# A third PSUM bank for the recurrences of the second segment, and B's serial products queued behind A's

## The chip, the core and the metric

The kernel runs on one core of a Trainium2 chip. The metric is the device time of one execution in microseconds (us), median of three runs. The core's engines work beside each other, each through a queue of its own and in the order in which its instructions stand there: TensorE (PE, matrix products; its weight loads are shown apart as PEld), VectorE (DVE), ScalarE (ACT), GpSimd (POOL), and SyncE (SP), which only issues transfers. PE writes its results to PSUM, eight banks of 128 x 512 f32; DVE and ACT empty them.

## The reference

A decoder block over 16 meta tokens and 1024 tokens of width 1024. `mm` stands for a product with weights, all in float32:

```python
h = concat(meta, x)
h = h + 0.5 * swiglu(rmsnorm(h), w_gu, w_down)             # D 1024, hidden 2816
u = rmsnorm(h)
aq, ak, av, az, beta, alpha, bcols, ga, gb = split(u @ w_in)
o_a = gated_delta(...)   # 8 heads of 128: per chunk  v_new = u - w S;  o = q S + attn v_new
                         #                            S = S * exp(g) + k^T v_new
o_b = rwkv7(...)         # 16 heads of 64: S = S * w + (S a) b + v k;   y = S r
h = h + (sigmoid(ga) * o_a + sigmoid(gb) * o_b) @ w_out
h = h + 0.5 * swiglu(rmsnorm(h), w_gu2, w_down2)
out = rmsnorm(h)[meta:]
```

A is the gated DeltaNet branch, B the RWKV-7 branch. Both carry a state from token to token; the kernel brings them to a form in which the state moves from chunk to chunk, 128 tokens for A and 64 for B.

## The kernel before

Three stages follow each other: `ffn1`, `middle` (from about 880 us to 2400 us of the span) and `ffn2`. Large products are made of three products of split operands (`mm3`): a projection tile `pp` of 128 x 512 takes 8 x 3 = 24 matmuls with a bank of PSUM, and its weights `w` come as `wraw` by a transfer and are split in two by ACT (L159) and DVE (L160). The small products of the recurrences are in plain f32; the trace shows each of those as two matmuls of half the length, with two weight loads.

`middle` runs two segments: the first of 528 tokens (the 16 meta tokens and 512), the second of 512. In each it takes eight pairs of heads, one of A with two of B. So there are 16 iterations, it 0 to 7 and 8 to 15. In an iteration the function `schedule` lists, in this order: `merge_blocks` and `transitions` (what B's chunks and the triangular inverses need, products iv, xp, vp, mp, np), `operands` of the next iteration (grb, gra, bkt, ktp), its inverse (62 small DVE steps, tb and Xb), `chains`, `gates` (projections zg, gs, gg and the product gat), `finish` (column sums cs, norms, merge), and `new_b` and `new_a` two iterations ahead (projections vB, kB, rB; column sums cs and bon; the meta tokens' transpose vbm in segment 1; convolutions acc). This is the programme's order only: a scheduler draws instructions from all these acts into each engine's queue, with the earlier act first where several are ready by its own reckoning. What stands in a queue is then fixed, and an instruction that waits holds all behind it. In the second half of it 6 the banks are dealt anew for segment 2 (`segment`), so the work from it 7 on runs with the second segment's banks.

The eight banks of `middle` are three pools: mm (projections), mx (operands and column sums of new work) and ch (`merge_blocks`, `transitions`, `chains` and `finish`'s column sums). ch has two banks throughout; mm has two tiles of two banks in segment 1 and three of one bank in segment 2; mx has the rest, two and three.

`chains` walks the states. For a chunk i of A: p1 (state times keys) goes to DVE, which makes rhA; p2 (inverse times rhA) goes to ACT, which makes vn; pq gathers two products, pq1 with the state and pq2 with vn, and ACT copies it to kq; p3 (keys times vn) goes to DVE, which makes the new state S (the tile SA). For a chunk of B: b (transition times state) goes to DVE, which makes the next state, a slice of SBs. Four chunks of A and eight of B follow one after another, and after them bq makes B's outputs of all chunks. Each product takes the next bank of ch, in program order; the next bank has to be empty. In the program before, the chunks stand as b0, A0, b1, b2, A1, b3, b4, A2, b5, b6, A3, b7.

`transitions` forms its products with `run`, which fills two tiles (even and odd chunks), each a bank: `mp` is emptied by DVE into mt (four steps, L1472) and AR (two, L1475), xp by ACT into xa, xv (L1464) and at, `np` by DVE into vbk and yb.

Of the kernel before, what the change touches and what calls it, by code (L numbers as in the profile page):

```python
# [13 lines left out]
P = 128  # L14
# [14 lines left out]
NCB = FULL // CB  # L29
CA = 128  # L30
NCA = FULL // CA
# [7 lines left out]
NJ = 8  # L39
WB = 2  # L40
AHEAD = 1
S1 = 3
HK = KD // 2
HF = NF // 2
NTMP = 8
# [61 lines left out]
def build(tc, nc, a):  # L107

    ctx = ExitStack()
    with ctx:  # L110
        g = K()
        g.tc, g.nc, g.a = tc, nc, a
        nc.scalar.preload_act_table_set("natural_log_exp_and_others")
        pad = ctx.enter_context(tc.tile_pool(name="pad", bufs=1, side="right"))
        nc.vector.memset(pad.tile([P, 24], F32, name="pad"), 0.0)
        const = ctx.enter_context(tc.tile_pool(name="const", bufs=1))
        wp = ctx.enter_context(tc.tile_pool(name="wp", bufs=2))
        dram = ctx.enter_context(tc.tile_pool(name="dram", bufs=1, space=bass.MemoryType.DRAM))
        g.mmctx = ctx.enter_context(ExitStack())
        main_banks(g, 2, 3, 8)  # L120
        g.const, g.wp, g.dram = const, wp, dram

        ones = const.tile([P, P], F32, name="ones")
        nc.gpsimd.dma_start(ones, a["ck"][:, :P])
        g.pk = const.tile([P, NPK], F32, name="pk")
        nc.gpsimd.dma_start(g.pk, a["pk"])

        def pv(n):
            o, w = PK[n]
            return g.pk[:, o : o + w]  # L130

        nc.vector.tensor_scalar(pv("omu"), pv("mu"), -1.0, 1.0, op0=ALU.mult, op1=ALU.add)
        nc.vector.tensor_scalar(pv("oka"), pv("ka"), -1.0, 1.0, op0=ALU.mult, op1=ALU.add)
        for n in ("w0", "a0"):
            nc.vector.tensor_scalar(pv(n), pv(n), -1.0, None, op0=ALU.mult)
        g.C = lambda n: ones if n == "ones" else g.ck[:, CK[n][0] - P : CK[n][0] - P + CK[n][1]]
        g.V = lambda n, i=0: g.pk[:, PK[n][0] + i : PK[n][0] + i + 1]

        hdr = [dram.tile([KD, P, sn], F32, name=f"hdr{s}") for s, (_, sn, _) in enumerate(SEGS)]
        mdr = [dram.tile([NJ, P, FULL], F32, name=f"mdr{s}") for s in range(2)]  # L140
        g.hdr, g.mdr = hdr, mdr
        g.sdr = dram.tile([NJ, P, P + CB], F32, name="sdr")
        g.gdr = [dram.tile([NJ, FULL], F32, name=f"gdr{s}") for s in range(2)]
        g.rdr = dram.tile([P, FULL], F32, name="rdr")
        g.h2dr = dram.tile([KD, P, FULL], F32, name="h2dr")
        g.h3dr = dram.tile([KD, P, FULL], F32, name="h3dr")
        g.hid = dram.tile([NF, P, T], F32, name="hid")

        g.worder, g.wready, g.wfetched, g.wused = list(weight_order()), [], 0, 0
        ffn1(g)  # L150
        middle(g)
        ffn2(g)
# [83 lines left out]
    return w  # L236


def main_banks(g, w, n, banks=6):

    g.mmctx.close()
    g.mmw = w
    pool = lambda name, bufs: g.mmctx.enter_context(
        g.tc.tile_pool(name=name, bufs=bufs, space=bass.MemoryType.PSUM, reuse_waits="tile"))
    g.mm = pool("mm", n)
    g.mx = pool("mx", banks - n * w)


def mm_tile(g, name, n=512, first=256):
# [462 lines left out]
def ffn2(g):  # L712
    tc, nc = g.tc, g.nc
    n = FULL
    main_banks(g, 1, 6, 8)
    with ExitStack() as ctx:
        right = ExitStack()
        bp = ctx.enter_context(tc.tile_pool(name="f2b", bufs=1, reuse_waits="tile"))
# [2 lines left out]
        with tc.tile_pool(name="f2n", bufs=1, reuse_waits="tile") as sp:  # L721
# [16 lines left out]
            w = next(q0), next(q1)  # L738
# [44 lines left out]
def middle(g):  # L783
    tc, nc = g.tc, g.nc
    g.mmctx.close()
    with ExitStack() as ctx:
        g.ch = ctx.enter_context(tc.tile_pool(name="ch", bufs=2, space=bass.MemoryType.PSUM, reuse_waits="tile"))
        ctx.callback(g.mmctx.close)
        ep = lambda name, bufs=1: ctx.enter_context(tc.tile_pool(name=name, bufs=bufs, reuse_waits="tile"))
        g.ms = ep("ms")  # L790
        g.st = ep("st")
        ms = g.ms
        g.carB = ms.tile([P, 27], F32, name="carB")
        g.carA = ms.tile([P, 24, 3], F32, name="carA")
        g.nrate = ms.tile([P, 1], F32, name="nrate")
        nc.scalar.activation(g.nrate[64:72], g.V("lr")[64:72], AF.Exp)
        nc.vector.tensor_scalar(g.nrate[64:72], g.nrate[64:72], -1.0, None, op0=ALU.mult)


        g.Y = [ms.tile([P, NT, P], F32, name=f"Y{i}") for i in range(2)]  # L800
        g.XA = ms.tile([CB, NCA, 2, 2, 16], F32, name="XA")
        g.Ub = ms.tile([115, 32, 32], F32, name="Ub")

        g.mt = ms.tile([P, NCB, P], F32, name="mt")
        for t in (*g.Y, g.XA, g.Ub, g.mt):
            nc.gpsimd.memset(t, 0.0)
        g.bkpm = ms.tile([P, 2, 64], F32, name="bkpm")
        nc.gpsimd.memset(g.bkpm, 0.0)
        g.bkm = ms.tile([P, 64], F32, name="bkm")
        nc.gpsimd.memset(g.bkm, 0.0)  # L810

        g.upz = ms.tile([P, 4, P], F32R, name="upz")
        nc.gpsimd.memset(g.upz.bitcast(F32), 0.0)
        g.uvm = [ms.tile([64, P], F32, name=f"uvm{i}") for i in range(2)]
        for t in g.uvm:
            nc.gpsimd.memset(t, 0.0)


        g.sums = {}
        for x in ("ones", "bd"):  # L820
            g.sums[x] = ms.tile([P, P], F32R, name=f"{x}r")
            nc.vector.tensor_copy(g.sums[x], g.C(x))
        steps = {}
        for act, it in schedule():
            if act == "segment":
                segment(g, it)
            elif act == "new_b":
                steps[it] = new_b(g, it)
            else:
                ACTIONS[act](g, steps[it])  # L830
# [24 lines left out]
def segment(g, s):  # L855

    nc = g.nc
    t0, n, off = SEGS[s]
    if s:
# [3 lines left out]
        for k in range(KD):  # L863
# [1 line left out]
            nc.sync.dma_start(hk[:, :n], g.hdr[s][k])  # L865
            nc.vector.scalar_tensor_tensor(hk[:, :n], hk[:, :n], g.V("gm", k), rs[:, :n], op0=ALU.mult, op1=ALU.mult)
            g.u.append(u_tile(g, hk[:, :n]))
    main_banks(g, *((1, S1) if s else (2, 2)))
    c = g.seg = K()
    c.s, c.n, c.off, c.u = s, n, off, g.u  # L870
    lora(g, c)
# [612 lines left out]
def chains(g, q):  # L1484
# [34 lines left out]
    def chunk_a(i):  # L1519
        csl = slice(i * CA, (i + 1) * CA)  # L1520
        p1 = pt("p1")
        nc.tensor.matmul(p1[:, :P], lhsT=kqg[:, 0, csl], rhs=S, start=True, stop=True)
        rh = st.tile([P, P], F32, name="rhA", tag="rhA", bufs=1)
        nc.vector.tensor_tensor(rh, Va[:, i, :], p1[:, :P], op=ALU.subtract)
        p2 = pt("p2")
        nc.tensor.matmul(p2[:, :P], lhsT=Y[:, NCB + i, :], rhs=rh, start=True, stop=True)
        vn = st.tile([P, P], F32, name="vn", tag="vn", bufs=2)
        nc.scalar.activation(vn, p2[:, :P], AF.Identity, scale=c.tk[:, i, j : j + 1])
        pq = pt("pq")
# [7 lines left out]

    SBs = st.tile([P, NCB + 1, CB], F32, name="SBs", tag="SBs")
    nc.gpsimd.tensor_copy(SBs[:, 0], SB)
    for i in range(NCB):  # L1540
        ps = pt("b1")
        nc.tensor.matmul(ps[:, :CB], lhsT=g.mt[:, i], rhs=SBs[:, i], start=True, stop=True)  # L1542
        nc.vector.scalar_tensor_tensor(SBs[:, i + 1], ps[:, :CB], q.gam[:, i : i + 1], q.vbk[:, i],
                                       op0=ALU.mult, op1=ALU.add)
        if i % 2 == 0:
            chunk_a(i // 2)
    ps = pt("bq")
    for i in range(NCB):
        for hp in HS:
# [146 lines left out]
```

## Time and profile before

| | us |
|---|---|
| three runs, median | 3086.55 (3084.68 to 3089.25) |
| profiled execution | 3085.29 |
| its span, first to last instruction | 3083.5 |
| PE busy | 2959.3 (96%) |
| DVE busy | 1976.2 (64%) |
| ACT busy | 1376.7 (45%) |
| POOL busy | 354.9 (12%) |

PE is busy nearly throughout, so the span is PE's work and the short stretches in which PE waits. Its clock was granted at 0.989 of full speed on average. Busy shares are means over stages that differ: DVE is busier in `middle` than before and after it.

### The profile page before, as it was taken

The numbers are of one execution on the slowest core, as the hardware profiler recorded it, in microseconds if no ns is written. First come the engines' busy times: TensorE is split into PE (matmuls) and PEld (weight loads), VectorE is DVE, ScalarE is ACT, GpSimd is POOL, SyncE is SP. The second block draws the span as 40 slices with busy tenths as digits, with TensorE's granted clock in tenths as the row PEclk, the third lists the DMA queues.
The fourth block names the chain that finished last, engine by engine and source line by source line (L and its number), as shares of the span: only waits on it lengthen the run. The fifth ranks groups of instructions, "written<-read, shape, count | busy, mean of one in ns | idle before, by whom it ended". The sixth has DMA issues, their size and how long they took to land.

```text
span 3083.5 us, 61656 instructions
## 1 busy us (share of the span) xinstructions
PE 2959.3 (96%) x25498; PEld 2539.0 (82%) x25498; DVE 1976.2 (64%) x3840; ACT 1376.7 (45%) x2404; POOL 354.9 (12%) x519
## 2 busy tenths in 40 slices
PE   8999999999899999999999999999999999999998
PEld 8999998998778888788777777777777888887886
DVE  6455454346677777787867877777866655555335
ACT  5322222126555656566566655665644432222114
POOL 0222220000001000001001000010100022222000
PEclk9999999999899999999999999999999999999999
DMA  3232224234222322333332332223354232224223
GB/s 125 82 97 83 83 86 158 79 101 140 62 74 73 79 70 59 85 79 75 97 89 73 84 81 75 75 75 84 109 148 165 68 104 94 83 83 170 86 78 114
DMA packets 257593, 287.19 MB, mean 93 GB/s; under 512 B 169296, under 2 KB 175440, under 8 KB 257312
## 3 DMA queue, kind: packets, MB, share of 16 engines
q1 hardware_dynamic: 253072, 271.43, 29.4%
q0 software_dynamic: 2512, 8.65, 0.7%
q8 instruction: 201, 3.29, 0.4%
q10 hardware_dynamic: 1728, 3.16, 0.3%
q14 instruction: 80, 0.66, 0.1%
HBM read 232.70 MB, written 50.47 MB: 92 GB/s over the span
## 4 chain that ended last, share of the span: by engine, by line
PE 54%; DVE 11%; ACT 7%; issue 2%; DMA 2%; SPq 0%; DVEq 0%; POOL 0%; ACTq 0%
PE pp L262 18%; PE pg L450 12%; PE pd L262 7%; PE pwo L262 3%; DVE w L160 1%; PE pg L474 1%; PE b L1542 1%; PE cs L1003 1%; PE gra L1252 1%; DMA ugr<-in_upg 1%; PE bkt L1281 1%; DVE tb L1364 1%; DVE mt L1472 1%; DVE Xb L1366 1%; PE vp L1056 1%
## 5 line engine op out<-in xcount | busy, mean ns | idle before, releaser
L262 PE MATMUL pp<-uk,w 128*128 128x512 f32 (+2 forms) x4824 | 975.1, 347 | 15.8 <-DVE w L160 9.3
L262 PEld LDWEIGHTS pp<-uk,w 128*128 128x128 f32 x4824 | 744.7, 191 | 109.1 <-DVE w L160 13.0
L159 ACT ACTIVATE w<-wraw 128x1024 fp32r<-128x1024 f32 (+2 forms) x330 | 326.3, 989 | 712.6 <-PE pd L262 287.6
L262 PE MATMUL pd<-hd,w 128*128 128x512 f32 (+2 forms) x2640 | 495.6, 349 | 11.3 <-DVE w L160 6.7
L262 PEld LDWEIGHTS pd<-hd,w 128*128 128x128 f32 x2640 | 427.5, 189 | 78.2 <-DVE w L160 8.6
L160 DVE TENSOR_TENSOR w<-wraw,w 128x1024 fp32r<-128x1024 f32 (+2 forms) x330 | 376.1, 1140 | 90.9 <-ACT w L159 85.7
L456 DVE TENSOR_TENSOR c<-c,pg 128x520 f32<-128x520 f32 (+1 forms) x280 | 189.2, 689 | 337.3 <-PE pg L450 278.3
L450 PE MATMUL pg<-bt,w 128*128 128x256 f32 (+2 forms) x2520 | 403.9, 317 | 0.0
L450 PEld LDWEIGHTS pg<-bt,w 128*128 128x128 f32 x2520 | 361.0, 188 | 32.9 <-DVE w L160 0.2
L450 PE MATMUL pg<-b,w 128*128 128x256 f32 (+2 forms) x2160 | 348.1, 317 | 0.2 <-DVE c L456 0.2
L450 PEld LDWEIGHTS pg<-b,w 128*128 128x128 f32 x2160 | 309.8, 188 | 28.5 <-PE pg L450 0.4
L419 POOL TENSOR_TENSOR wrx<-wrx 128x512 f32<-128x512 f32 x38 | 57.2, 1505 | 755.1 <-DVE w22b L160 515.3
L1364 DVE TENSOR_TENSOR tb<-Ub,Xb 115x126 f32<-115x126 f32 (+22 forms) x496 | 124.1, 250 | 11.0 <-DMA Ub<-scr 2.7
L1366 DVE TENSOR_TENSOR Xb<-Xb,tb 115x126 f32<-115x126 f32 (+22 forms) x496 | 125.3, 253 | 8.7
L159 ACT ACTIVATE w<-wrx 128x1024 fp32r<-128x1024 f32 (+1 forms) x64 | 58.1, 908 | 156.8 <-PE pg L450 152.3
L1173 DVE SCALAR_TENSOR_TENSOR acc<-xr,pk,acc 128x528 f32<-128x528 f32 (+1 forms) x144 | 109.0, 757 | 26.4 <-ACT acc L1169 25.3
L609 DVE SCALAR_TENSOR_TENSOR h<-pd,h 128x528 f32<-128x528 f32 (+1 forms) x64 | 44.6, 698 | 115.0 <-PE pd L262 115.0
L609 DVE SCALAR_TENSOR_TENSOR hh<-pd,hh 128x512 f32<-128x512 f32 x64 | 44.2, 690 | 109.7 <-PE pd L262 106.6
L262 PE MATMUL pwo<-uk,w 128*128 128x512 f32 x384 | 101.5, 414 | 4.2 <-DVE w L160 1.9
L262 PEld LDWEIGHTS pwo<-uk,w 128*128 128x128 f32 x384 | 73.6, 197 | 22.2 <-DVE w L160 2.7
L923 ACT ACTIVATE sh<-pp,pk 128x528 f32<-128x528 f32 (+1 forms) x54 | 37.5, 694 | 98.3 <-PE pp L262 98.3
L159 ACT ACTIVATE hd<-hr 128x1040 fp32r<-128x1040 f32 (+1 forms) x44 | 45.3, 1061 | 68.6 <-DMA hr<-hid 43.7
(397 smaller groups left out, 4143.1 us busy)
## 6 DMA issues: line engine op xcount, KB each, us to landing
wraw<-in_win SPq DMA_DIRECT2D x150, 512.0 KB
wraw<-in_wgu SPq DMA_DIRECT2D x44, 512.0 KB
wrx<-in_wgu SPq DMA_DIRECT2D x44, 512.0 KB
wraw<-in_wdn SPq DMA_DIRECT2D x48, 320.0 KB
wraw<-in_wdn SPq DMA_DIRECT2D x32, 384.0 KB
hid<-c SPq DMA_DIRECT2D x44, 260.0 KB
hr<-hid SPq DMA_DIRECT2D x22, 520.0 KB
hid<-c SPq DMA_DIRECT2D x44, 256.0 KB
```

Source lines behind the costliest of these rows:

```text
L159: g.nc.scalar.activation(hi, src, AF.Copy)
L160: (eng or g.nc.vector).tensor_tensor(lo, src, hi.bitcast(F32), op=ALU.subtract)
L262: g.nc.tensor.matmul(ps, lhsT=l, rhs=r, start=i == 0, stop=i == n - 1)
L419: sums.tensor_tensor(a22, a21, a22, op=ALU.add)
L450: nc.tensor.matmul(ps[:, c0 : c0 + cn], lhsT=l[:, x, k, :], rhs=r[:, k, y, c0 : c0 + cn], start=i == 0, stop=i == 3 * HK - 1)
L456: nc.vector.tensor_tensor(o, x, y, op=ALU.add)
L474: nc.tensor.matmul(ps[:, c0 : c0 + cn], lhsT=l[:, x, k, :], rhs=r[:, k, y, c0 : c0 + cn], start=i == 0, stop=i == 6 * HK - 1)
L609: nc.vector.scalar_tensor_tensor(hv, pd, 0.5, hv, op0=ALU.mult, op1=ALU.add)
L923: nc.scalar.activation(sh[:, 1 : 1 + n], ps, AF.Identity, scale=g.V("mu", i))
L1173: nc.vector.scalar_tensor_tensor(acc[:, :n], xr[:, tap : tap + n], V("convw", ct * 4 + tap), acc[:, :n], op0=ALU.mult, op1=ALU.add)
L1364: nc.vector.tensor_tensor(tv, U[:, i, i + 1 :].unsqueeze(2).to_broadcast([npt, nt, ncc]), X[:, i, 0:ncc].unsqueeze(1).to_broadcast([npt, n ...
L1366: nc.vector.tensor_tensor(X[:, i + 1 :, 0:ncc], X[:, i + 1 :, 0:ncc], tv, op=ALU.add)
```

## The change

Three things are edited. The ch pool is made in `main_banks`, with mm and mx, and so can differ by segment. In segment 2 it gets three banks, and mm two (`S1` 3 to 2); segment 1 keeps two tiles of mm, two banks of mx and two of ch, in other places. In `chains` the body of B's loop becomes `chunk_b`, and the chunks' products are put by `issue_after`: b of chunk 2i directly behind p1 of A's chunk i, b of chunk 2i+1 directly behind p2. No product and no transfer is added or taken away.

```diff
--- before.py
+++ after.py
@@ -39,7 +39,7 @@
 NJ = 8
 WB = 2
 AHEAD = 1
-S1 = 3
+S1 = 2
 HK = KD // 2
 HF = NF // 2
 NTMP = 8
@@ -117,7 +117,7 @@
         wp = ctx.enter_context(tc.tile_pool(name="wp", bufs=2))
         dram = ctx.enter_context(tc.tile_pool(name="dram", bufs=1, space=bass.MemoryType.DRAM))
         g.mmctx = ctx.enter_context(ExitStack())
-        main_banks(g, 2, 3, 8)
+        main_banks(g, 2, 3)
         g.const, g.wp, g.dram = const, wp, dram
 
         ones = const.tile([P, P], F32, name="ones")
@@ -236,14 +236,16 @@
     return w
 
 
-def main_banks(g, w, n, banks=6):
+def main_banks(g, w, n, ch=0):
 
     g.mmctx.close()
     g.mmw = w
     pool = lambda name, bufs: g.mmctx.enter_context(
         g.tc.tile_pool(name=name, bufs=bufs, space=bass.MemoryType.PSUM, reuse_waits="tile"))
     g.mm = pool("mm", n)
-    g.mx = pool("mx", banks - n * w)
+    g.mx = pool("mx", 8 - n * w - ch)
+    if ch:
+        g.ch = pool("ch", ch)
 
 
 def mm_tile(g, name, n=512, first=256):
@@ -712,7 +714,7 @@
 def ffn2(g):
     tc, nc = g.tc, g.nc
     n = FULL
-    main_banks(g, 1, 6, 8)
+    main_banks(g, 1, 6)
     with ExitStack() as ctx:
         right = ExitStack()
         bp = ctx.enter_context(tc.tile_pool(name="f2b", bufs=1, reuse_waits="tile"))
@@ -784,7 +786,6 @@
     tc, nc = g.tc, g.nc
     g.mmctx.close()
     with ExitStack() as ctx:
-        g.ch = ctx.enter_context(tc.tile_pool(name="ch", bufs=2, space=bass.MemoryType.PSUM, reuse_waits="tile"))
         ctx.callback(g.mmctx.close)
         ep = lambda name, bufs=1: ctx.enter_context(tc.tile_pool(name=name, bufs=bufs, reuse_waits="tile"))
         g.ms = ep("ms")
@@ -865,7 +866,7 @@
             nc.sync.dma_start(hk[:, :n], g.hdr[s][k])
             nc.vector.scalar_tensor_tensor(hk[:, :n], hk[:, :n], g.V("gm", k), rs[:, :n], op0=ALU.mult, op1=ALU.mult)
             g.u.append(u_tile(g, hk[:, :n]))
-    main_banks(g, *((1, S1) if s else (2, 2)))
+    main_banks(g, *((1, S1, 3) if s else (2, 2, 2)))
     c = g.seg = K()
     c.s, c.n, c.off, c.u = s, n, off, g.u
     lora(g, c)
@@ -1519,11 +1520,15 @@
     def chunk_a(i):
         csl = slice(i * CA, (i + 1) * CA)
         p1 = pt("p1")
-        nc.tensor.matmul(p1[:, :P], lhsT=kqg[:, 0, csl], rhs=S, start=True, stop=True)
+        m = nc.tensor.matmul(p1[:, :P], lhsT=kqg[:, 0, csl], rhs=S, start=True, stop=True)
         rh = st.tile([P, P], F32, name="rhA", tag="rhA", bufs=1)
         nc.vector.tensor_tensor(rh, Va[:, i, :], p1[:, :P], op=ALU.subtract)
+        with g.tc.issue_after(m.ins):
+            chunk_b(2 * i)
         p2 = pt("p2")
-        nc.tensor.matmul(p2[:, :P], lhsT=Y[:, NCB + i, :], rhs=rh, start=True, stop=True)
+        m = nc.tensor.matmul(p2[:, :P], lhsT=Y[:, NCB + i, :], rhs=rh, start=True, stop=True)
+        with g.tc.issue_after(m.ins):
+            chunk_b(2 * i + 1)
         vn = st.tile([P, P], F32, name="vn", tag="vn", bufs=2)
         nc.scalar.activation(vn, p2[:, :P], AF.Identity, scale=c.tk[:, i, j : j + 1])
         pq = pt("pq")
@@ -1537,13 +1542,15 @@
 
     SBs = st.tile([P, NCB + 1, CB], F32, name="SBs", tag="SBs")
     nc.gpsimd.tensor_copy(SBs[:, 0], SB)
-    for i in range(NCB):
+
+    def chunk_b(i):
         ps = pt("b1")
         nc.tensor.matmul(ps[:, :CB], lhsT=g.mt[:, i], rhs=SBs[:, i], start=True, stop=True)
         nc.vector.scalar_tensor_tensor(SBs[:, i + 1], ps[:, :CB], q.gam[:, i : i + 1], q.vbk[:, i],
                                        op0=ALU.mult, op1=ALU.add)
-        if i % 2 == 0:
-            chunk_a(i // 2)
+
+    for i in range(NCA):
+        chunk_a(i)
     ps = pt("bq")
     for i in range(NCB):
         for hp in HS:
```

The scheduler draws the whole order of `middle` anew. Three places show what changes.

The first is PE's queue in it 12, in `chains`: one chunk of A with its two chunks of B. Before:

```order
L1542 MATMUL b_23890<-SBs,mt 128x64 [waits Activation_49]
L262 MATMUL pp<-uk,w 128x512 x4
L1542 MATMUL b_23893<-SBs,mt 128x64 [waits DVE_49]
L1522 MATMUL p_23896<-SA,kq 128x128
L262 MATMUL pp<-uk,w 128x512 x3
L1526 MATMUL p_23900<-rhA,Y_7138 128x128 [waits DVE_49]
L1530 MATMUL pq<-kq,SA 128x128
L262 MATMUL pp<-uk,w 128x512 x2
L1531 MATMUL pq<-attn,vn 128x128 [waits Activation_49]
L1533 MATMUL p_23907<-vn,ktl 128x128
L262 MATMUL pp<-uk,w 128x512
```

And now:

```order
L1523 MATMUL p_23897<-SA,kq 128x128 [waits DVE_49,Activation_49]
L1548 MATMUL b_23901<-SBs,mt 128x64
L264 MATMUL pp<-uk,w 128x512 x2
L1529 MATMUL p_23904<-rhA,Y_7135 128x128 [waits DVE_49]
L1548 MATMUL b_23906<-SBs,mt 128x64 [waits DVE_49]
L1535 MATMUL pq<-kq,SA 128x128
L264 MATMUL pp<-uk,w 128x512
L1536 MATMUL pq<-attn,vn 128x128 [waits Activation_49]
L1538 MATMUL p_23914<-vn,ktl 128x128
L264 MATMUL pp<-uk,w 128x512 x3
```

There were four visits between projections (b; b and p1; p2 and pq1; pq2 and p3), now there are three. Counted over the sixteen iterations, such visits are 263 before (118 up to it 6, 145 from it 7 on) and 221 now (112 and 109). The projections between p1 and p2 are two instead of three.

The second is PE's queue in it 12, at the end of `transitions`, where grb and gra are operands of the next iteration. Before:

```order
L1056 MATMUL mp<-BKt,xa 64x64 [waits Activation_49]
L1056 MATMUL mp<-BKt,xa 64x64 x7
L1056 MATMUL mp<-LT,xa 64x64 x12
L1211 MATMUL grb<-AR,BK 64x128 x15
L262 MATMUL pp<-uk,w 128x512 x2
L1056 MATMUL np<-xv,BKt 64x64 [waits DVE_49,PE_49]
L1056 MATMUL np<-xv,BKt 64x64 x2
L1056 MATMUL np<-xv,BKt 64x64 [waits DVE_49,PE_49]
L1056 MATMUL np<-xv,BKt 64x64 x12
L1056 MATMUL np<-LT,xv 64x64 x16
L1211 MATMUL grb<-AR,BK 64x128 [waits DVE_49]
L1211 MATMUL grb<-AR,BK 64x128 x7
```

And now:

```order
L1057 MATMUL mp<-BKt,xa 64x64 [waits Activation_49]
L1057 MATMUL mp<-BKt,xa 64x64 x7
L1057 MATMUL mp<-LT,xa 64x64 x13
L1057 MATMUL np<-xv,BKt 64x64 [waits Activation_49]
L1057 MATMUL np<-xv,BKt 64x64 x7
L1057 MATMUL np<-LT,xv 64x64 x8
L1212 MATMUL grb<-AR,BK 64x128 x8
L1057 MATMUL np<-xv,BKt 64x64 [waits DVE_49,PE_49]
L1057 MATMUL np<-xv,BKt 64x64 x7
L1057 MATMUL np<-LT,xv 64x64 x8
L1212 MATMUL grb<-AR,BK 64x128 x11
```

The first half of np, which had stood with the second behind fifteen grb and two projections, stands directly behind mp; eight grb separate the halves.

The third is PE's queue in it 7, from the last column sum of `finish` and `new_b` to bon and beyond, where the queue of `new_a` follows. Before:

```order
L1003 MATMUL cs<-hl,bdr 128x512
L262 MATMUL pp<-uk,w 128x512 x4
L1003 MATMUL cs<-hl,bdr 128x512
L262 MATMUL pp<-uk,w 128x512 x27
L1003 MATMUL bon<-hl,bdr 128x512 x2
L262 MATMUL pp<-uk,w 128x512 x17
L1003 MATMUL cs<-hl,onesr 128x512
L262 MATMUL pp<-uk,w 128x512 x4
L1003 MATMUL cs<-hl,onesr 128x512
L262 MATMUL pp<-uk,w 128x512 x18
```

And now:

```order
L1004 MATMUL cs<-hl,bdr 128x512
L264 MATMUL pp<-uk,w 128x512 x3
L1004 MATMUL cs<-hl,bdr 128x512
L264 MATMUL pp<-uk,w 128x512 x5
L1004 MATMUL bon<-hl,bdr 128x512
L264 MATMUL pp<-uk,w 128x512 x3
L1004 MATMUL bon<-hl,bdr 128x512
L264 MATMUL pp<-uk,w 128x512 x31
L1004 MATMUL cs<-hl,onesr 128x512
L264 MATMUL pp<-uk,w 128x512 x5
```

Between the end of `chains` (bq) and the first bon product stood 58 projection matmuls, now 35; behind it come 17, now 3 and 31, until the next column sum. On DVE's queue three weight splits (L160) stood between the first rhA of it 7 and bv, of which bon's operand is made; now one.

In segment 1, its 1 to 7, vbm stood on PE behind vbp and two projection matmuls of 272 columns; now it stands behind vbp and eight of them.

## Rows read from the trace of the kernel before

**Rows 1.** The page's first part: busy us (share) and instructions.

```profile
PE 2959.3 (96%) x25498; PEld 2539.0 (82%) x25498; DVE 1976.2 (64%) x3840; ACT 1376.7 (45%) x2404; POOL 354.9 (12%) x519
```

**Rows 2.** PE's waits, whole run: waiting line <- releaser: us in total, times, longest.

```profile
PE np L1056 <- DVE AR L1475: 14.1, 15, 2.3
...
PE vbm L1118 <- ACT Vs L1115: 6.3, 8, 1.0
PE vp L1056 <- ACT xv L1464: 6.0, 14, 0.6
...
PE p L1526 <- DVE rhA L1524: 2.2, 1, 2.2
```

**Rows 3.** Its 8 to 14 as one window: us, busy by engine, PEclk, DMA.

```profile
core 0: us, PE busy (x) PEld busy (x) DVE busy (x) ACT busy (x) POOL busy (x), PEclk, DMA share, GB/s
1681.18:2284.11 602.93, 579.78 (x6497) 463.90 (x6496) 479.49 (x1131) 354.32 (x680) 48.45 (x104) 1.00 0.33 88
```

**Rows 4.** Waits of line 1542 (b), whole run: releaser, us, times.

```profile
  ACT kq L1535: 10.7, 47
```

**Rows 5.** Timeline of it 12, one A chunk: start, us, instruction, idle before.

```profile
2146.34 0.30 PEld L1542 LDWEIGHTS b<-SBs,mt 128*128 128x128 f32 x2 [0.23 <-ACT kq L1535]
...
2146.59 1.17 PE L262 MATMUL pp<-uk,w 128*128 128x512 f32 x4
...
2147.60 0.33 PE L1542 MATMUL b<-SBs,mt 128*128 128x64 f32 x2
...
2147.77 0.44 PE L1522 MATMUL p<-SA,kq 128*128 128x128 f32 x2
...
2147.96 0.94 PE L262 MATMUL pp<-uk,w 128*128 128x512 f32 x3
...
2148.24 0.29 DVE L1524 TENSOR_TENSOR rhA<-Va,p 128x128 f32<-128x128 f32 x1
...
2149.10 0.71 PE L262 MATMUL pp<-uk,w 128*128 128x512 f32 x2
2149.16 0.37 ACT L1528 ACTIVATE vn<-p,tk 128x128 f32<-128x128 f32 x1 [2.86 <-PE p L1526]
...
2150.43 0.43 PE L1542 MATMUL b<-SBs,mt 128*128 128x64 f32 x2
```

**Rows 6.** Timeline of PE, segment 1, around vbm.

```profile
1324.83 4.39 PE L262 MATMUL pp<-uk,w 128*128 128x272 f32 x35
...
1331.29 0.39 PE L1118 MATMUL vbm<-ck,vB 128*16 128x128 f32 x2 [1.00 <-ACT Vs L1115]
```

**Rows 7.** Timeline of it 12, end of the transitions.

```profile
2133.39 1.73 DVE L1472 TENSOR_TENSOR mt<-mp,ck 64x256 f32<-64x256 f32 x4 [0.21 <-PE mp L1056]
...
2135.14 0.76 DVE L1475 TENSOR_TENSOR AR<-mp,AR 128x256 f32<-128x256 f32 x2
...
2135.71 0.86 PE L1056 MATMUL np<-xv,BKt 64*64 64x64 f32 x26 [0.47 <-DVE AR L1475]
...
2137.15 1.09 PE L1211 MATMUL grb<-AR,BK 64*64 64x128 f32 x16
```

**Rows 8.** It 7: PE's waits from 1640 to 1681.18, and a window.

```profile
PE pp L262 <- DVE w L160: 2.8, 1, 2.8
PE pp L262 <- ACT acc L1169: 1.7, 1, 1.7
...
1659.00:1671.00 12.00, 8.49 (x21) 5.71 (x22) 11.20 (x26) 6.15 (x11) 2.27 (x2) 0.57 0.33 92
```

**Rows 9.** Timeline of it 12, readers of the projection zg.

```profile
2118.11 0.60 ACT L932 ACTIVATE zg<-pp 128x512 f32<-128x512 f32 x1 [0.22 <-PE pp L262]
...
2121.86 0.69 DVE L1570 TENSOR_TENSOR zg<-pp,zg 128x512 f32<-128x512 f32 x1 [1.07 <-ACT zg L934]
```

**Rows 10.** Timeline of PE, a column sum of `new_b`.

```profile
2182.94 0.50 PE L1003 MATMUL cs<-hl,bdr 128*128 128x512 f32 x1 [0.56 <-DVE hl L1018]
```

**Rows 11.** Timeline of PE, it 15, `finish`.

```profile
2324.76 5.21 PE L262 MATMUL pwo<-uk,w 128*128 128x512 f32 x22
...
2331.45 0.50 PE L1003 MATMUL cs<-hl,onesr 128*128 128x512 f32 x1 [1.25 <-DVE hl L1018]
```

## The prediction

> **What bounds the kernel now.** I read the page first: TensorE (PE) is busy 2959.3 of 3083.5 us, so all idle time of PE is 124 us [rows 1]. No time can be won but out of those 124 us, or out of busy time in which PE only looks busy. The second view is PE's waits over the whole run [rows 2]. The largest is the second pair of transition products, np, which waits for VectorE (DVE) to empty the mp banks: 14.1 us in 15 waits. The meta transpose vbm waits 6.3 us in 8, vp for xv 6.0 us in 14, p2 for rhA once 2.2 us. The other serial products that the change reorders (p1, b, pq, p3) are not among the large ones. Third, one window over seven iterations of the second segment [rows 3]: PE 579.8 of 602.9 us, DVE 479.5. The idle part is 23.2 us, 3.3 us an iteration; DVE has 20% of air on average.
>
> The fourth view changes the picture: the waits by line, for b's line alone. Its weight loads stood idle 10.7 us, 47 times, until ScalarE's (ACT) copy kq had emptied pq's bank [rows 4]. That is 0.23 us each, and it hides in PE's busy time, since the matmul ahead is drawn longer. The timeline of one A chunk shows it [rows 5]: the lone b's weights load at 2146.34 after 0.23 us of idle.
>
> **The serial products.** In [rows 5] one A chunk with its two b runs from 2146.34 to 2150.43, 4.09 us, and holds 10 projection matmuls (four, three, two and one). Those go at 5.21/22 = 0.237 us [rows 11], so 2.37 us; the chain's seven products take the other 1.72 us in four visits (b; b p1; p2 pq1; pq2 p3). By the order three visits remain. A lone b costs 0.25 us (2146.34 to 2146.59) plus its wait of 0.23; a b beside another product costs 0.17 (2147.60 to 2147.77), and two waits of 0.23 come per chunk at most. So a visit taken away is worth between 0.25 - 0.17 = 0.08 and 0.25 + 0.23 - 0.17 = 0.31 us. The orders have 263 visits before and 221 after (36 of the 42 in its 7 to 15). 42 x 0.08 = 3.4, 42 x 0.31 = 13. Against it: the new order leaves fewer projections between dependent products. rhA is ready at 2148.53, 0.57 us behind p1's slot (2147.77 to 2147.96), and behind p1 there will stand b (0.17) and two projections (0.47) where three projections stand now: nearly no slack. Ahead of pq2, where vn takes 0.37 us, one projection remains in every second chunk. DVE and ACT serve in order, so anything ahead of rhA or vn on their queues now shows on PE. I take 0.15 us a visit, **-6.3**, and 0.08 us a chunk of new waits, 32 chunks and more, **+2.3**: together **-4**, between 0 and -13.
>
> A rule of the Trainium skill bears on this: "Perfetto Trace Analysis", section "Matmuls", wants independent matmul groups to rotate through different PSUM banks, so that one is emptied while the next runs. It speaks for three recurrence banks and against two projection banks; the 47 waits agree, and taken alone it would make the first of these two sums the full 10.7 us.
>
> **Vbm, segment 1 (its 1 to 7).** vbm waits 1.00 us with two 272-column matmuls behind vbp [rows 6]; the new order puts eight there. Six more at 4.39/35 = 0.125 us cover 0.75. Seven waits of at most 0.75 are 5.3; nothing if PE then only meets its next wait sooner. I take **-4** (0 to -6.3).
>
> **Transitions with three banks (its 7 to 15).** Now np waits until DVE is through both mp tiles: mt 1.73 us from 2133.39, AR until 2135.90; PE has fifteen grb and two projections ahead of it and still waits 0.47 us there [rows 7], 0.94 on average (14.1/15). After, np's first half has a free bank and goes directly behind mp, then eight grb, then the second half. Half of np is 1.44/2 = 0.72 us (2135.71 to 2137.15), eight grb at most 1.09 us. The second half's bank is free when four mt and one AR are done, 1.73 + 0.38 = 2.1 us behind mp: 0.3 to 0.7 us of wait remain. Nine times (0.94 less 0.7) is 2.2; the end is nine times 0.94, 8.5. I take **-2.5**. vp's wait for xv goes (6.0 us over 14, 0.43 each, nine times 3.9), but mp stands behind the same evictions: **-1**, 0 to -3.9. p2's single 2.2 us stands at a place whose order changes: **-1.5**.
>
> **Two projection banks.** A projection tile may stay until the next but one starts, 24 x 0.237 = 5.7 us and the serial products between. The slowest reader shown is zg: projection done by 2118.11, DVE through at 2121.86 + 0.69, 4.4 us [rows 9]. So it is hidden; if DVE is 1.3 us later, PE stands still. **+1**, 0 to +10 (seven iterations of 1.5).
>
> **It 7, the switch.** Here DVE is the bound: in these 12 us it is busy 11.2, PE 8.5, and the granted clock is 0.57, so most of them pass at 1.2 GHz [rows 8]. PE waits 1.7 us for acc and 2.8 us for a weight split; the inverse's small steps alternate on DVE with all the rest. The change shortens the chain, so PE is at bon after 35 projections behind bq instead of 58: 23 x 0.237 = 5.5 us earlier, while bon needs the same DVE chain, relieved of two weight splits only. PE then stands at bon, and has 34 projections behind its first product instead of 17, ahead of the next column sum. What PE was ahead is lost here, and the low clock can last longer. I take **+3**, -5 to +12.
>
> **Give-back.** From it 8 on, the column sums of new_b already wait for DVE, 0.56 us at 2182.94 [rows 10]; PE that comes 1 us earlier waits for some of it. About 0.3 us in each of seven iterations, **+2** (0 to +6). At the end the first column sum of the last finish waits 1.25 us between its two halves [rows 11]; the tail loses its serial visits and has more output projections ahead of the first of them: **-1.2**.
>
> Sum: -4 -4 -2.5 -1 -1.5 +1 +3 +2 -1.2 = **-8.2 us**. The profiled execution takes 3085.3 us, 1.8 over its span; that gives 3077.1. The median of the three runs, 3086.55, is 1.25 above it: **3078**. 0.2%, 6.2 us, is about what a measurement of this kernel can tell from no change, so faster is below 3080.4 and slower above 3092.7.
>
> **Rivals.** (a) *The gain is given back.* DVE's new_b chain and the inverse set the period; PE only meets cs, bon and the splits earlier. For it: DVE's 80% and the waits of [rows 10]; against it: PE's 96%. The give-back then takes its bound of 6, the two-bank term 3: -8.2 + 4 + 2 = -2.2, 3084, and 3087 where three of the chain's four go too. This includes that the change does not do what it says, as p1, b and p3 show no wait to remove. Chance 0.26.
>
> (b) *Slower: projections starve on two banks.* Its place is it 7 and the gates, where DVE reads late. It decides when a tile's last reader ends more than 5.7 us behind its projection. Price: +12 in it 7, and 1.5 us in seven iterations, +10, against the other terms, -12.2: 3086.5 + 22 - 12.2 = 3096. Against it: segment 1 runs on two tiles already, with no such wait in [rows 2]. Chance 0.17. The clock stands at 0.57 in the row with these waits [rows 8]. The Trainium skill, "TensorE: Matmul & The Clock Gate", section "A second HAM failure mode: psum-queue depth-cycling", says that cycling through banks makes PE idle briefly between groups until its clock oscillates; by that, more changes of bank would cost clock throughout, but this trace holds 1.00 over the seven iterations [rows 3], so it is part of (b) only.
>
> (c) *Three times the gain.* The hidden 10.7 us go in full (-6.7 more), and it 7's two waits (4.5 us) with its low clock (12 us at 0.57, 5 us) too, -9.5 in place of +3: 3086.5 - 8.2 - 6.7 - 12.5 = 3059. For it: it 7's order changes much; against: DVE's load there stays. Chance 0.11. My forecast has 0.46.
>
> **Range.** 3064 to 3094: it leaves out most of (c) and the upper half of (b), 0.18 in all; the forecast's own range is 3071 to 3083. Faster: (c) and 0.41 of the forecast, 0.52; same: the rest of the forecast and (a), 0.31; slower: (b), 0.17.
>
> **What would show it.** Right: b's idle for kq near zero in its 8 to 15 and A chunks of 3.9 us for ten projections; vbm's wait under 0.3 us; np's below 0.7 us. It 7: a wait at bon of 4 us or more. Wrong: a new entry of PE waiting for a pp bank (its readers zg, vB, acc), or p2, pq2 and p1 together over 5 us; or seven iterations that take their 602.9 us as before.

## The result: slower, 1.0034 of before

The changed kernel takes 3099.56 us (median of 12 runs, 3092.64 to 3105.56); the kernel before took 3088.91 in the runs beside it. The ratio is 1.0034, 95% interval 1.0023 to 1.0045: slower by about 11 us, outside the predicted range and on the other side. The profiled execution is the slowest of the twelve, 3105.56 us with a span of 3103.8. So changes of the whole time are taken from medians, and a size read from a trace below is that of one execution.

PE's waits over the whole run of the changed kernel, longest first, against [rows 2] (lines are shifted by one to seven):

```profile
PE np L1057 <- DVE AR L1476: 15.8, 15, 2.5
...
PE pp L264 <- ACT acc L1170: 6.0, 1, 6.0
...
PE pp L264 <- ACT w L159: 3.9, 2, 2.0
PE mp L1057 <- ACT xv L1465: 3.6, 8, 0.7
PE tkp L980 <- DVE c L966: 3.4, 1, 3.4
...
PE vp L1057 <- ACT xv L1465: 2.6, 7, 0.4
PE vbm L1119 <- ACT Vs L1116: 2.5, 8, 0.6
```

vbm's wait fell from 6.3 to 2.5, p2's 2.2 is gone. np's did not fall, and vp's wait for xv moved to mp, 6.2 for both together where it was 6.0. New or larger are the waits for weights (`w`, ACT's half), for tkp, and for acc: PE waits in it 7 for a projection bank until ACT has made acc of it, 6.0 us once where it was 1.7 [rows 8].

The serial products did what the change says. The waits of b's line, and the timeline of one A chunk of it 13, against [rows 4, 5]:

```profile
  issue: 1.3, 6
```

```profile
2161.41 0.38 PE L1523 MATMUL p<-SA,kq 128*128 128x128 f32 x2
2161.63 0.33 PE L1548 MATMUL b<-SBs,mt 128*128 128x64 f32 x2
2161.77 0.71 PE L264 MATMUL pp<-uk,w 128*128 128x512 f32 x2
2162.32 0.38 PE L1529 MATMUL p<-rhA,Y 128*128 128x128 f32 x2
2162.54 0.33 PE L1548 MATMUL b<-SBs,mt 128*128 128x64 f32 x2
...
2165.29 0.38 PE L1523 MATMUL p<-SA,kq 128*128 128x128 f32 x2
```

The 10.7 us of idle for kq are 0, and the chunk, from one p1 to the next, runs 3.88 us with its ten projection matmuls (two, three and five) where it ran 4.09.

The loss is seen in the windows by iteration. Its 11 to 14 of the changed kernel (us, busy by engine, PEclk):

```profile
1943.36:2036.32 92.96, 86.45 (x941) 68.74 (x940) 70.82 (x165) 53.01 (x101) 10.39 (x16) 0.96 0.30 77
2036.32:2124.64 88.32, 84.81 (x941) 68.42 (x940) 70.38 (x166) 52.35 (x101) 9.25 (x16) 1.00 0.30 81
2124.64:2217.30 92.66, 86.00 (x942) 68.47 (x941) 70.82 (x165) 53.03 (x101) 7.32 (x16) 0.98 0.29 76
...
1686.62:2306.76 620.14, 587.12 (x6531) 472.95 (x6530) 483.38 (x1134) 357.74 (x687) 50.61 (x104) 0.99 0.33 87
```

It 11 and it 13 take 4 to 5 us more than it 12, and the seven iterations take 620.1 us against 602.9 in [rows 3] (with 6531 matmuls in them for 6497, since the border of it 8 moved; 34 at 0.237 us are 8 us of this, so on equal work they are about 9 us longer). The timeline of it 13, where ACT, DVE and PE meet:

```profile
2180.97 0.62 ACT L1097 ACTIVATE sw<-Ls 128x512 f32<-128x512 f32 x1
2181.49 0.62 ACT L1100 ACTIVATE ELx<-Ls 128x512 f32<-128x512 f32 x1
2182.01 1.05 ACT L159 ACTIVATE w<-wraw 128x1024 fp32r<-128x1024 f32 x1
...
2183.11 0.73 PE L264 MATMUL pp<-uk,w 128*128 128x512 f32 x2 [1.96 <-ACT w L159]
...
2184.06 0.68 DVE L1607 TENSOR_TENSOR yb<-yb,kq 128x512 f32<-128x512 f32 x1
...
2184.86 1.22 DVE L160 TENSOR_TENSOR w<-wraw,w 128x1024 fp32r<-128x1024 f32 x1
...
2186.14 4.15 PE L264 MATMUL pp<-uk,w 128*128 128x512 f32 x10 [2.29 <-DVE w L160]
```

PE has done everything up to new_b's second projection, whose weights are not split. ACT's half stands behind new_b's steps sw and ELx, and PE waits 1.96 us; DVE's half stands behind the four yb steps of `finish` (the last at 2184.06), PE waits 2.29 more. It 11 has the same pair, and these two have a granted clock of 0.96 and 0.98 where it 12 has 1.00. Why the split is late there shows in the place of gg, the last projection of `gates`. `w` has two buffers (`WB = 2`), so the weights of new_b's second projection can be split only when gg's products are done. Before, in it 13, gg was done ahead of bq, and both halves followed it closely:

```profile
2154.48 0.60 ACT L932 ACTIVATE gg<-pp 128x512 f32<-128x512 f32 x1 [0.18 <-PE pp L262]
2154.97 1.05 ACT L159 ACTIVATE w<-wraw 128x1024 fp32r<-128x1024 f32 x1
...
2156.73 1.22 DVE L160 TENSOR_TENSOR w<-wraw,w 128x1024 fp32r<-128x1024 f32 x1
```

In the changed kernel gg ends behind bq:

```profile
2172.83 0.60 ACT L933 ACTIVATE gg<-pp 128x512 f32<-128x512 f32 x1 [0.73 <-PE pp L264]
```

ACT starts on the split 9.2 us after this, DVE 12.0 us after it. That is theory T below: the shorter serial part takes fewer projections with it, gg is left for the stretch behind bq, and there the next weights' split is late.

### The profile page after: what moved, and what is told of

Its sections match the earlier page's. It is cut to its first block, busy times and chain, and to the rows that moved or that the text cites. A ratio compares the mean times of both kernels' runs of the same rounds, so it can differ in the third digit from the quotient of the medians.

```text
span 3103.8 us, 61694 instructions
## 1 busy us (share of the span) xinstructions
PE 2968.0 (96%) x25498; PEld 2553.4 (82%) x25498; DVE 1978.3 (64%) x3840; ACT 1375.8 (44%) x2404; POOL 358.7 (12%) x519
## 4 chain that ended last, share of the span: by engine, by line
PE 73%; DVE 13%; ACT 8%; issue 3%; DMA 3%; SPq 1%; POOL 0%; DVEq 0%; ACTq 0%; POOLq 0%
PE pg L452 24%; PE pp L264 15%; PE pd L264 15%; PE pg L476 3%; PE pwo L264 3%; DVE w L160 2%; DVE Xb L1367 1%; DVE tb L1365 1%; ACT w L159 1%; PE gra L1253 1%; PE cs L1004 1%; DVE mt L1473 1%; PE bkt L1282 1%; PE grb L1212 1%; PE vp L1057 1%
## 5 line engine op out<-in xcount | busy, mean ns | idle before, releaser
L160 DVE TENSOR_TENSOR w<-wraw,w 128x1024 fp32r<-128x1024 f32 (+2 forms) x330 | 376.0, 1140 | 86.1 <-ACT w L159 80.4
```

The lines of the kernel that those rows point to most:

```text
L160: (eng or g.nc.vector).tensor_tensor(lo, src, hi.bitcast(F32), op=ALU.subtract)
```

## The experiments

Ratios are to the kernel before, run beside each, with 95% intervals.

### Which part of the change

**The banks alone** (new banks, old order of products):

```diff
-        with g.tc.issue_after(m.ins):
-            chunk_b(2 * i)
...
-    for i in range(NCA):
-        chunk_a(i)
+    for i in range(NCB):
+        chunk_b(i)
+        if i % 2 == 0:
+            chunk_a(i // 2)
```

> The banks alone: second segment with three banks for the recurrences and two for projections, B's products in the old order b0 A0 b1 b2 A1. Theory T (the loss comes from weight splits: the shortened serial part on TensorE moves projections behind bq, where the split of the next weights stands on ScalarE and VectorE behind finish and new_b; it needs both parts of the change): no waits of 2 us for a weight split in its 11 and 13, time within 4 us of before, about 3086 to 3093. Rival R1 (two projection banks are too few): this run has them, so most of the loss, 3096 to 3101. Rival R2 (the new order of products lowers the clock): no loss, clock as before, 0.989.

3087.26 us, 0.9991 (0.9982 to 1.0001): no change. This speaks for T, and against R1: two projection banks lose nothing with the old order.

**The order alone** (two recurrence and three projection banks):

```diff
-S1 = 2
+S1 = 3
-    main_banks(g, *((1, S1, 3) if s else (2, 2, 2)))
+    main_banks(g, *((1, S1, 2) if s else (2, 2, 2)))
```

> The order alone: B's products directly behind p1 and p2, with two banks for the recurrences and three for projections in the second segment. Segment 1 is then the same program as in the changed kernel. Theory T: the serial part stays longer, since the banks hold it up, no split waits of 2 us in its 8 to 14; within 4 us of before, 3085 to 3093. R1: no loss, 3080 to 3088. R2: the loss is here, clock near 0.986, 3094 to 3101, part of it already in segment 1.

3082.42 us, 0.9979 (0.9970 to 0.9988): faster, somewhat more than T expected. R2 falls, since its loss should be here. What is left of R1 is that two projection banks are too few for the new order.

**A third projection bank** beside three for the recurrences, taken from mx:

```diff
-S1 = 2
+S1 = 3
```

> The changed kernel with the eight banks of the second segment dealt otherwise: three for projections, three for the recurrences, two for the operands and column sums. Theory T: VectorE's queue still has a weight split behind Ls and all four yb steps in two of its iterations, so those waits stay, 3094 to 3102. R1: the third projection bank takes the loss back, 3080 to 3090. R2: 3096 to 3101.

3102.01 us, 1.0045 (1.0032 to 1.0058). The wait for acc is 3.7 us with it for 6.0, but the time is not lower, so R1 is unlikely as the main cause. It is not excluded: the bank came from mx, and a loss for want of it there could hide a gain. The trace has one late split (it 11), not the two that were expected. Neither part of the change loses by itself; the two together do.

**The order in segment 2 alone**, on the banks of before:

```diff
+        if not meta:
             with g.tc.issue_after(m.ins):
                 chunk_b(2 * i)
```

(so for both products, and the old loop for segment 1.)

> The new order of B's products in the second segment alone, with the banks of the kernel before (two for the recurrences, three for projections). If the gain of the order alone (3082 against 3088) comes from the second segment, as its iterations 9 to 13 that were 0.5 to 4 us shorter say: 3080 to 3085. If it comes from the shorter wait of vbm in segment 1: 3086 to 3090.

3078.89 us, 0.9975 (0.9964 to 0.9985): the fastest full kernel here. The new order pays in segment 2. Whether it costs anything in segment 1 is not settled: 3082.42 less 3078.89 is 3.5 us, but the intervals of the two ratios overlap. The place where the changed kernel loses ahead of segment 2's regular iterations is the switch, its 6 and 7; the changed kernel and the one before:

```profile
1453.62:1686.62 233.00, 212.18 (x2041) 166.38 (x2040) 171.55 (x385) 137.58 (x258) 22.64 (x39) 0.95 0.30 82
```

```profile
1453.39:1681.18 227.79, 212.03 (x2072) 166.13 (x2072) 173.04 (x387) 140.92 (x265) 19.90 (x39) 0.98 0.31 85
```

That is 5.2 us more, at a clock of 0.95 against 0.98. But the window now holds 31 matmuls fewer; they are projections that stand behind the border, in it 8. At 0.237 us each they are 7.3 us, so on equal work its 6 and 7 are about 12.6 us longer, more than the 9 of its 8 to 14. The waits for tkp and acc from the list above and the low clock are part of it. Reckoned in the same way, these two iterations are about 10 us longer than before with the banks alone (231.66 us, 2046 matmuls) and with the order alone (233.51, 2053), but only 2 in the fastest kernel (229.64, 2072). These are single executions, and no run here takes this loss out by itself.

### The late split

**Fetched and split earlier**: new_b's second weights are taken at the end of `gates`, and so stand ahead of `finish` in program order:

```diff
+    if g.worder[g.wfetched]:
+        fetchw(g)
     ps = mm_tile(g, "gat")
```

> The changed kernel, and the weights of new_b's second projection are fetched and split one act earlier in program order, at the end of gates, ahead of finish; nothing else. Theory T: the waits of 2.0 and 2.3 us for the split in its 11 and 13 go, with the low clock behind them, 5 to 7 us each: 3085 to 3093. R1 and R2: no change, 3096 to 3102.

3088.85 us, 1.0009 (1.0000 to 1.0019): 10.7 us below the changed kernel by the medians, 7.7 by the two ratios, whose intervals do not meet. It 11 and it 13 are 88.82 and 87.04 us (92.96 and 92.66 above); the longest wait for weights in them is 0.2 us.

**The same in the kernel before**, the control:

> The kernel before with the earlier fetch and split of new_b's second weights (as was done to the changed kernel), a control. Theory T: no such wait exists here, so nothing comes of it, 3084 to 3091. If the earlier fetch is a gain of its own, whatever the order: 3075 to 3081.

3092.01 us, 1.0021 (1.0012 to 1.0029): slower by some 4 us, a little outside what T expected. So the earlier fetch is no gain of its own.

**And in the order alone**:

> The order alone (two banks for the recurrences, three for projections) with the earlier fetch and split. Theory T: as the order alone, 3079 to 3086, as no late split stands there. If the earlier fetch is a gain of its own: 3070 to 3077.

3084.35 us, 0.9993 (0.9984 to 1.0001), as T expected.

**The late split put into the kernel before**, in its 11 and 13:

```diff
+    m = nc.vector.tensor_tensor(yb, yb, oa, op=ALU.add)
+    g.late = m.ins if q.it in (11, 13) else None
...
+        if late is not None:
+            after.enter_context(g.tc.issue_after(late))
         w = loadw(g, "win", ct)
```

> The kernel before, with one thing put in its way: in its 11 and 13 VectorE's half of the split of new_b's second weights is queued behind the last of the four yb steps of finish, as it stands in the changed kernel. Theory T (late splits are the loss): TensorE waits 4 us or more for that split twice, the low clock may follow, 3096 to 3104. Rival R3 (such a wait is taken back at the next wait for VectorE, and the loss of the changed kernel lies elsewhere): 3086 to 3091.

3100.99 us, 1.0045 (1.0031 to 1.0059): 13.4 us more than before. The waits of it 11 and it 13 (one view each), and their windows:

```profile
PE pp L262 <- ACT w L159: 2.5, 2, 1.5
```

```profile
PE pp L262 <- ACT w L159: 1.6, 1, 1.6
```

```profile
1934.46:2027.59 93.13, 87.29 (x942) 68.90 (x941) 71.15 (x165) 52.83 (x101) 6.23 (x16) 0.98 0.29 77
...
2115.35:2205.67 90.32, 85.39 (x941) 67.99 (x940) 71.22 (x165) 53.87 (x103) 7.08 (x16) 1.00 0.28 76
```

The waits are shorter than the 4 us expected, and they are not for the late split. The scheduler drew the order anew and, as the halves of the splits show, put new_b's third projection (rB) ahead of its second (kB). In it 11:

```profile
1993.48 0.73 PE L262 MATMUL pp<-uk,w 128*128 128x512 f32 x2 [0.96 <-ACT w L159]
...
1994.39 1.21 DVE L160 TENSOR_TENSOR w<-wraw,w 128x1024 fp32r<-128x1024 f32 x1
1995.66 11.87 PE L262 MATMUL pp<-uk,w 128*128 128x512 f32 x44 [0.64 <-DVE w L160]
...
1998.23 0.69 DVE L1604 TENSOR_TENSOR yb<-yb,kq 128x512 f32<-128x512 f32 x1
1999.01 1.22 DVE L160 TENSOR_TENSOR w<-wraw,w 128x1024 fp32r<-128x1024 f32 x1
...
2008.13 0.75 DVE L928 SCALAR_TENSOR_TENSOR kB<-pp,pk,sh 128x512 f32<-128x512 f32 x1 [2.35 <-ACT sh L927]
```

PE waits for a split that stands ahead of the yb steps, and runs 44 projection matmuls across the one behind them (1999.01) without a break. What is late is kB, at 2008.13 where the kernel before had it at 1998.54, and with it the steps that read it. It 13 is alike. So this run does not put the changed kernel's wait into the kernel before, and leaves R3 undecided; it shows that the kernel with these splits behind the yb steps is 13 us slower, though PE is given other work meanwhile. The two iterations are 5.5 and 3.1 us longer than the 87.65 and 87.27 of before, in an execution (3093.96) that was this kernel's fastest. How the rest of the 13.4 us splits into waits, clock and moved work is not resolved.

**With three projection banks**, the earlier fetch on top of the 3, 3 and 2:

> Three banks for the recurrences, three for projections, two for operands (3102), with the earlier fetch and split of new_b's second weights; no iteration has a late split then. Theory T: 8 to 14 less, 3088 to 3094, as with two projection banks. If the late split was only worth something with two projection banks: 3099 to 3104.

3095.57 us, 1.0022 (1.0013 to 1.0031): 6.4 us less, short of the 8 to 14. The late split, of which that kernel has one, counts there too, but is not all.

**Segment 1 back in the old order**, three banks and new order in segment 2 only (the edit of the fastest kernel, applied to the changed one):

> The changed kernel with segment 1 in the old order of products, so the new order and the three banks act in the second segment only. In its order a late weight split (behind all four yb steps of finish) stands in three iterations (9, 11, 13), where the changed kernel has two. Theory T with some 5 us for each: 3099.6 less the 3.5 that the old order in segment 1 gave at two banks, and 5 more: 3097 to 3105. If segment 1 were the main loss: 3084 to 3092.

3110.27 us, 1.0063 (1.0051 to 1.0076): slower than I expected. There are three iterations with a late split, and all three are long:

```profile
1761.92:1856.62 94.70, 87.28 (x941) 70.00 (x940) 70.84 (x164) 53.01 (x101) 10.71 (x16) 0.96 0.29 74
1944.42:2037.08 92.66, 85.98 (x942) 68.51 (x941) 70.78 (x165) 53.01 (x101) 10.28 (x16) 0.98 0.30 76
2125.45:2218.12 92.67, 86.00 (x941) 68.51 (x940) 70.82 (x165) 53.03 (x101) 10.04 (x16) 0.98 0.29 76
```

**The same with the earlier fetch**:

> The same, with the earlier fetch and split of new_b's second weights; no iteration then has a late split. Theory T: 3082 to 3089, some 15 below the same kernel without the fetch. Whatever stays above the order alone in the second segment (3079) belongs to three recurrence and two projection banks themselves.

3099.74 us, 1.0033 (1.0021 to 1.0045). The fetch takes 10.5 us away again, but 10 us stay above before, and the 15 less that I expected were not there. Its 9 and 10 are long here (88.87 and 87.51 us in the changed kernel); their waits, and the windows:

```profile
PE np L1057 <- DVE AR L1476: 5.5, 2, 3.2
```

```profile
1771.29:1861.33 90.04, 85.54 (x942) 69.15 (x941) 71.70 (x166) 53.40 (x102) 8.24 (x16) 0.98 0.30 81
1861.33:1953.58 92.25, 85.75 (x942) 69.28 (x941) 69.91 (x163) 52.82 (x101) 6.67 (x16) 0.96 0.28 75
```

Here np waits 2.3 and 3.2 us for DVE, and the clock falls behind each of them. More of the 10 us stands at the switch: on equal work its 6 and 7 (231.40 us, 2046 matmuls) are about 10 us longer than before, its 8 to 14 (612.83, 6523) about 4. So the late split is not the only loss. That with three banks PE runs up to DVE, and meets as a wait whatever stands badly in DVE's queue, fits these windows; it was not tested.

### Does VectorE take the gain back?

**The last two yb steps on GpSimd**, in the changed kernel, and in the fastest:

```diff
-    nc.vector.tensor_tensor(yb, yb, gg, op=ALU.mult)
-    nc.vector.tensor_tensor(yb, yb, oa, op=ALU.add)
+    nc.gpsimd.tensor_tensor(yb, yb, gg, op=ALU.mult)
+    nc.gpsimd.tensor_tensor(yb, yb, oa, op=ALU.add)
```

> The changed kernel with the last two of the four yb steps of finish (times gg, plus oa) on GpSimd in place of VectorE, 1.4 us an iteration less there. If VectorE takes back what the serial products save and holds the late split: 3081 to 3092, with less idle time before np, cs and w. If the two projection banks or the low clock are the loss: 3096 to 3103.

3107.64 us, 1.0058 (1.0046 to 1.0070).

> The new order in the second segment alone with the banks of before (3079), and the same two steps on GpSimd. No late split stands here and the waits for VectorE are short, so little is to be won: 3074 to 3081. A gain of 5 us or more would say that VectorE holds this kernel too.

3110.73 us, 1.0070 (1.0057 to 1.0083). Both are slower, both against every theory. The inverse's steps by line, whole run, with GpSimd's steps and without them (the fastest kernel):

```profile
L1365 DVE TENSOR_TENSOR tb<-Ub,Xb 115x126 f32<-115x126 f32 (+22 forms) x496 | 137.1, 276 | 13.8 <-DMA Ub<-scr 4.7
L1367 DVE TENSOR_TENSOR Xb<-Xb,tb 115x126 f32<-115x126 f32 (+22 forms) x496 | 136.2, 275 | 9.1
```

```profile
L1367 DVE TENSOR_TENSOR Xb<-Xb,tb 115x126 f32<-115x126 f32 (+22 forms) x496 | 125.4, 253 | 8.4
L1365 DVE TENSOR_TENSOR tb<-Ub,Xb 115x126 f32<-115x126 f32 (+22 forms) x496 | 124.5, 251 | 12.3 <-DMA Ub<-scm 2.9 <-DMA Ub<-scr 1.2
```

```profile
L1613 POOL TENSOR_TENSOR yb<-yb,gg 128x512 f32<-128x512 f32 x16 | 36.4, 2278 | 142.7 <-DVE yb L1612 89.4 <-issue 53.3
```

The steps took DVE 0.68 us each, 22 us in all; GpSimd needs 2.28 for the first, and DVE's small steps grow by 23.4 us. The growth stands beside GpSimd's steps:

```profile
1742.38 2.49 POOL L1613 TENSOR_TENSOR yb<-yb,gg 128x512 f32<-128x512 f32 x1 [8.78 <-DVE yb L1612]
...
1743.75 1.19 DVE L1365 TENSOR_TENSOR tb<-Ub,Xb 115x56 f32<-115x56 f32 x1
...
1746.35 0.21 DVE L1365 TENSOR_TENSOR tb<-Ub,Xb 115x45 f32<-115x45 f32 x1
```

Of the 992 small steps, the 55 that ran at the same time as one of GpSimd's yb steps took 0.70 us on average, the other 937 took 0.25. DVE was not relieved, so the runs say nothing of the question.

**The same two steps left out** (so the result lacks the gate and A's part), in the changed kernel, the fastest, and the one before:

> The changed kernel without the last two yb steps of finish (times gg, plus oa; that part of the result is left out): 1.4 us an iteration less on VectorE and nothing put on GpSimd. If VectorE holds the kernel with three banks: 3080 to 3090, 10 to 20 below the changed kernel. If it doesn't: 3094 to 3101.

3084.11 us, 0.9983 (0.9974 to 0.9992).

> The new order in the second segment alone with the banks of before (3079), without the same two steps of finish. If TensorE's own work holds it: 3073 to 3079. If VectorE holds it as well: 3060 to 3070.

3079.16 us, 0.9968 (0.9957 to 0.9980).

> The kernel before without the same two steps of finish, the measure for the two runs that leave them out: 3080 to 3088 if TensorE holds it, 3065 to 3075 if VectorE does.

3080.44 us, 0.9972 (0.9961 to 0.9982). The same 22 us of DVE's work are worth 15.5 us in the changed kernel, 8.4 in the one before and nothing measurable in the fastest. But the scheduler draws the order anew in each, and in the changed kernel without the two steps its 11 and 13 no longer have a late split: they take 85.86 and 87.50 us for 92.96 and 92.66. That may be most of the 15.5. So which kernel DVE's load holds most is not shown.

## Why the prediction was wrong

The step that failed is **Give-back**, "About 0.3 us in each of seven iterations, +2", and with it the view that projections behind bq fill PE at no cost. It has two parts, and a third loss comes from **It 7**, whose +3 was too small.

First, the serial products: PE's saving there was right, and larger than said. Two iterations without late split and at full clock (it 12 and 13), of the kernel before, of the changed one with the earlier fetch, and of the order alone in segment 2:

```profile
2022.11:2196.49 174.38, 169.55 (x1882) 136.04 (x1881) 140.46 (x328) 105.82 (x203) 15.22 (x32) 1.00 0.31 82
```

```profile
2029.75:2203.91 174.16, 166.08 (x1882) 135.15 (x1881) 140.67 (x328) 105.08 (x203) 18.96 (x32) 1.00 0.30 82
```

```profile
2017.64:2190.61 172.97, 168.67 (x1881) 136.48 (x1881) 139.99 (x328) 105.07 (x203) 14.59 (x32) 1.00 0.31 82
```

With three banks PE is busy 166.08 us for the same products, 3.5 less than before; the time is only 0.2 less. The rest became idle time, 1.6 us an iteration, most of it at np, which waits 2.5 us for DVE (1.0 before), and the column sums, 1.9 (1.1). With two banks PE saves 0.9 and keeps it, 1.4 us shorter. I had 2 us of give-back for the whole segment; in these two iterations it is 1.6 us each, nearly all that three banks and the new order saved. The rival (a) named this mechanism, and priced it too low.

Second, the split of weights. I looked at splits on DVE only in it 7, and did not ask where the next split stands when gg ends behind bq. Taken away, it gives 10.7 us (7.7 by the ratios) in the changed kernel and 10.5 in the one with segment 1 in the old order, while the same edit gains nothing in two kernels without a late split. With it gone the changed kernel is where the kernel before was. No term of the sum had it; rival (a) names the splits, without a price. Its tell was in the order: four yb steps, then `w`, in its 11 and 13.

Third, the switch: its 6 and 7 lose about 12.6 us on equal work in the profiled execution, where the term had +3 and 12 as its bound. The chain that it gave was another: PE waits 1.1 us at bon, not 4 or more, but 3.4 for tkp and 6.0 for acc, at a clock of 0.95 for 0.98. The banks alone and the order alone lose 10 there too, so the cause is not one part of the change; it stays open.

Of the signs named, b's idle and the chunk of 3.9 us came as forecast, and so did the sign against it, a longer wait for acc. np's mean wait, 15.8/15 = 1.05 us, did not fall below 0.7.

The other terms:

- **Vbm, -4**: the wait fell by 3.8 us. But its 0 to 5 of segment 1 take 572.6 us where they took 572.9, the clock 0.99 for 1.00: no gain is left.
- **Transitions, -2.5 and -1**: wrong. np's halves with eight grb between still meet DVE's mt and AR, 15.8 us for 14.1, and mp waits for what vp waited for.
- **p2's 2.2 us, -1.5**: gone, as said.
- **Two projection banks, +1**: low. PE waits 4.3 us more for acc, in it 7, where rival (b) had put it, and 0.7 once for gs; a third bank takes 2.3 of this back, and with the order alone, on three banks, the wait is 3.6 as well. The iterations between show no such wait. So the time came close to that rival's 3096, mostly by another cause.
- **The end, -1.2**: the 1.25 us within the first column sum went; one wait of 2.8 us before the second stands there now. Between the start of it 15 and the end the changed kernel won 2.4 us (22.7 late at 2306.76, 20.3 at the end).

The parts do not add up to 11 us: the order gains 8.7 in segment 2, and the whole change loses 11; taking out the late splits brings back 8 to 11, and the switch shows a loss of its own that gains elsewhere make up for. Open, beside the switch, is why segment 1's old order with three banks is 11 us slower than with the new one (3110.27 against 3099.56, 3099.74 against 3088.85): the waits that it has moved to its 9 and 10 were seen, but what puts them there was not tried.

## What to carry to other kernels

Taking waits out of a serial part on the busiest engine pays only as far as the next engine's queue allows: look at what the filler work needs (here a split of weights on two other engines), where that stands in their queues, and what will arrive earlier. Where a scheduler draws the order anew, try the parts of a change apart, and look in the trace whether the edit did what it was meant to; here the new order in segment 2 alone is worth 9 us, and the whole change loses 11. Windows that are cut at an instruction can hold different work: count it before their lengths are compared. A queue's order that puts a short step, for which the busiest engine will wait, behind a long run of others can be found before any run.

## What was not expected of the hardware

GpSimd's elementwise steps slowed VectorE's: 496 pairs of small steps went from 251 and 253 ns to 276 and 275 on average when 32 steps ran on GpSimd, all of it in the 55 that ran beside one of them, so the move returned nothing. The Trainium skill says as much in "Perfetto Trace Analysis", section "Optimizing Scalar/DVE Operations": the two share a read port of SBUF, so moving operations between them may not help. This trace agrees.

The clock: in each of the five iterations that show the two waits of about 2 us for weights (its 11 and 13 of the changed kernel, its 9, 11 and 13 with segment 1 in the old order) the granted clock is 0.96 to 0.98, and it is 1.00 in it 11 and it 13 with the earlier fetch. One such wait did not always do this: np's 2.5 us in it 9 of the changed kernel left it at 1.00. The pair costs more than its 4.3 us: 92.7 us against 87.0 in it 13.
